# Modulation steps, two weight splits and a memset put elsewhere, and a second power in each layer norm

## Chip, cores and metric

The kernel runs on one core of a Trainium2 chip. The metric is the device time of one execution in microseconds, median of three runs. TensorE (PE) multiplies, with weight loads on PEld; VectorE is DVE, ScalarE is ACT, GpSimd is POOL, and SP is the queue that issues most loads.

## What is computed

Two layers of a first transformer block on 256 tokens of 1024 values, then two layers of a second block on its result and on 256 context tokens. Cut to what matters here, a layer of the first block is:

```python
mod = c_act @ ada_w[l] + ada_b[l]
sh1, sc1, g1, sh2, sc2, g2 = jnp.split(mod, 6, axis=-1)
h = _modulate(x, sh1, sc1)                 # norm of x, times 1 + sc1, plus sh1
mix = _hybrid_mixer(h, ...)                # h @ w_in, attentions, convolution, @ w_o
x = _layer_norm(ALPHA * x + (1.0 + g1) * mix, ln1_g, ln1_b)
h = _modulate(x, sh2, sc2)
ffn = _peer(h, ...)                        # 16384 experts, U and V tables, gates from top-16
x = _layer_norm(ALPHA * x + (1.0 + g2) * ffn, ln2_g, ln2_b)
```

The second block computes its own modulation rows in the same way, from its own `w_ada`.

## The kernel before

A matrix product is made of three products of halves in a rounded fp32 format. `wtile` (line 272) loads a raw weight tile (`raw`, five buffers) on SP and calls `split` (260): ScalarE copies the high half (`wh`, 262), VectorE subtracts it for the low half (`wl`, 264); there are five buffers of each. `mm3` (295 to 297) makes the three products. The code is one program order; a scheduler orders each engine's and each queue's instructions from it by priority (program order) and by its own model of times, so an instruction may be drawn far forward into what the model takes for idle time. On the chip each engine and queue then runs in that fixed order. `tc.issue_after(ins)` holds the instructions made under it behind `ins` on that engine; `PIN` passes such a bound to `split`.

Modulation rows are made in two ways. `ada` (323) multiplies on PE (L342) from loads `adaw` (L334) with four buffers. `ada_v` (381) runs on VectorE: for each of eight row blocks a load (L392, two buffers) and a scaled sum into `adacc` (L396 for the first, L398 for the others), then a finish: a sum over partitions on PE (L404) into the one bank that `ada` uses too, the bias (L412), transposes (L421) and a copy (L425). Each block and the finish are a step of a generator. `behind` (460) holds eleven such parts: one of layer 0, six of layer 1, four of the second block. Its `run(budget)` adds to a debt and takes steps, each worth 1.0, while the debt is above zero.

`peer` (817) computes the experts. Its second half is a loop over V (1033): 64 positions of two experts, first 120 to 126, then 0 to 118 in steps of two. Each position multiplies activations and gates on VectorE (1038), splits them and two V tiles of 1024 columns, and makes 24 products into `acc`, one pair of banks for each of the two token blocks. At the end of each position stands `behind.run`. In layer 0 the products of the last two positions are put off and made token block by token block, so that `resid_ln` (554) can start on the first. `resid_ln` takes for each block: gate (557), residual (558), `ln_stats` (468), two scaled operations (560, 561) into X.

`ln_stats` takes bn_stats of two halves (471), bn_aggr (473), the epsilon (475), and `power` (463), which is a pow on GpSimd (465). There are 16 layer norms in the program: eight in `resid_ln` and eight in `make_hT`.

After `peer(0)` comes `mixer(1)` (565). It clears `krn` (595) and calls `make_hT` (495) for each block: `ln_stats`, `neg_mul` (487, kept as `LATE["dve"]`), xn on ScalarE (509), transposes on PE (515), hf (519, 521) and its split into hh and hl. Then the products `pn` with `w1n` follow (608 to 614), eight row blocks each split at columns 416 and 256, and the products of `ada(2, 0, 0)` are handed out in program order behind them. `krn` is written from L628 on, behind `pn`.

Of the kernel before, what the change touches and what calls it, by code (L numbers as in the profile page):

```python
# [205 lines left out]
def kernel(ctx: ExitStack, tc: tile.TileContext, a: dict, out: bass.AP):  # L206
    nc = tc.nc
    V, SC, T, G, SP = nc.vector, nc.scalar, nc.tensor, nc.gpsimd, nc.sync
# [8 lines left out]
    def pool(name, side=None):  # L217
        return tc.tile_pool(name=name, bufs=1, side=side, reuse_waits="tile")
# [12 lines left out]
    def bank(shape, name, tag):  # L231
        return PP[0].tile(shape, F32, name=name, tag=tag, bufs=PP[1][tag])
# [5 lines left out]
    def cst(name, t=None):  # L238
        o, n = CW[name]
        return (k1 if t is None else t)[:, o:o + n]  # L240

    ident, iota = cst("ident"), cst("iota")
    def x_tile():
        return const.tile([128, 2, D], F32, name="x", tag="x8", bufs=1)
# [10 lines left out]
    def raw_tile(src, shape):  # L255
        r = ring.tile([128] + shape, F32, name="raw", tag="raw", bufs=RAW)
        SP.dma_start(r, src)
        return r

    def split(dst_h, dst_l, src):  # L260
        with after(PIN.get("act")):
            SC.activation(dst_h, src, AF.Copy)  # L262
        with after(PIN.get("dve")):
            return V.tensor_tensor(dst_l, src, dst_h, op=OP.subtract).ins  # L264

    LAST = [None]
    PIN = {}

    def after(ins):
        return tc.issue_after(ins) if ins else ExitStack()  # L270

    def wtile(src, shape, cuts=None, keep=None):


        r = raw_tile(src, shape)
        parts = []
        c0 = 0
        for cut in cuts or [shape[0] // 2] * 2:
            sh = [cut] + shape[1:]
            h, lo = [(keep or ring).tile([128] + sh, F32R, name=nm, tag=nm, bufs=4 if keep else NHL) for nm in ("wh", "wl")]  # L280
            LAST[0] = split(h, lo, r[:, c0:c0 + cut])
            parts.append((h, lo))
            c0 += cut
        return parts
# [9 lines left out]
    def mm3(o, lh, ll, rh, rl, first, last):  # L294
        T.matmul(o, lh, rh, start=first, stop=False)  # L295
        T.matmul(o, lh, rl, start=False, stop=False)  # L296
        T.matmul(o, ll, rh, start=False, stop=last)  # L297
# [139 lines left out]
    def mod_row(dst, blk, l, part, s=0):  # L437
        SP.dma_start(dst, bcast_row(mod(blk, l, part, s), D))
# [21 lines left out]
    behind = Filler(*[ada_v(*key) for key in [(1, 0, 5)] + [(1, 1, i) for i in range(6)] + [(2, 1, i) for i in range(2, 6)]])  # L460


    def power(var, u=""):
        r = small.tile(list(var.shape), F32, name="rstd", tag=f"rstd{var.shape[-1]}{u}")
        G.tensor_tensor(r, var, cst("half").to_broadcast(list(var.shape)), op=OP.pow)
        return r

    def ln_stats(xt, u=""):
        st = small.tile([128, 2, 6], F32, name="st" + u)
        for h in range(2):  # L470
            V.bn_stats(st[:, h], xt[:, 512 * h:512 * h + 512])
        mv = small.tile([128, 2], F32, name="mv" + u)
        V.bn_aggr(mv, st)
        v = small.tile([128, 1], F32, name="ve" + u)
        V.tensor_scalar(v, mv[:, 1:2], LN_EPS, None, op0=OP.add)
        return mv[:, 0:1], power(v, u)
# [6 lines left out]
    LATE = {}  # L483
# [11 lines left out]
    def make_hT(work, xt, kind, scc, shc, hh, hl, t0, tag, bufs=2, act=False):  # L495

        xn = work.tile([128, D], F32, name="xn", tag="xn", bufs=bufs)
        if kind == "ln":
            m, r = ln_stats(xt, "h")
            nb = neg_mul(m, r)  # L500
        else:
            ss = small.tile([128, 1], F32, name="ssh")
            SC.activation(xn, xt, AF.Square, accum_out=ss)
            r = rms_from(ss, D, "h")
        hf = work.tile([128, KB, 128], F32, name="hf", bufs=bufs)
        for h in range(2):
            c = slice(512 * h, 512 * h + 512)
            if kind == "ln":
                LATE["act"] = SC.activation(xn[:, c], xt[:, c], AF.Identity, scale=r, bias=nb).ins
            else:  # L510
                V.tensor_scalar(xn[:, c], xt[:, c], r, None, op0=OP.mult)
            pt = bank([128, 4, 128], "hTp", tag)
            for j in range(4):
                k = 4 * h + j
                LATE["pe"] = T.transpose(pt[:, j], xn[:, 128 * k:128 * k + 128], ident).ins
            for j in range(4):
                k = 4 * h + j
                if j % 2 or act:
                    SC.activation(hf[:, k], pt[:, j], AF.Identity, scale=scc[:, k:k + 1], bias=shc[:, k:k + 1])
                else:  # L520
                    V.tensor_scalar(hf[:, k], pt[:, j], scc[:, k:k + 1], shc[:, k:k + 1], op0=OP.mult, op1=OP.add)
            k = slice(4 * h, 4 * h + 4)
            split(hh[:, k, t0:t0 + 128], hl[:, k, t0:t0 + 128], hf[:, k])
        return hf
# [40 lines left out]
    def mixer(l):  # L565
# [19 lines left out]
        with pool(f"mix{l}") as p:  # L585
# [6 lines left out]
            sbv = p.tile([128, 2, 256], F32, name="sbv")  # L592
            qln = p.tile([128, 2, 384], F32, name="qln")
            krn = p.tile([128, 2, 128], F32, name="krn")
            V.memset(krn, 0.0)
            proj = {n: p.tile([128, 2, S], F32, name="t" + n) for n in ("sq", "sk", "cb", "cc")}
            order = ("cb", "cc", "ch", "sq", "sk")
            ph = sth.enter_context(pool(f"mixh{l}"))
# [2 lines left out]
            with pool(f"mixx{l}") as px:  # L601
                for tb in range(2):
                    make_hT(px, X[0][:, tb], "ln", sc, sh, hh, hl, 128 * tb, "m")
            pat = sth.enter_context(pool(f"mixa{l}"))


            pn = [[bank([128, 512], f"pn{tb}{c}", "m") for c in range(2)] for tb in range(2)]
            for k in range(KB):
                w = wtile(a["w1n"][l, 128 * k:128 * k + 128, :], [672], (416, 256))
                for tb in range(2):  # L610
                    t = slice(128 * tb, 128 * tb + 128)
                    for c, n in enumerate((416, 256)):
                        mm3(pn[tb][c][:, :n], hh[:, k, t], hl[:, k, t], w[c][0][:, :n], w[c][1][:, :n],
                            k == 0, k == KB - 1)
# [107 lines left out]
            for hp in range(2):  # L722
                h = slice(2 * hp, 2 * hp + 2)
# [64 lines left out]
            with banks(f"o{l}", pm=2), pool(f"mixo{l}") as p:  # L788
# [9 lines left out]
                for i, k in enumerate(korder):  # L798
                    w = p.tile([128, 2, 2, 512], F32R, name=f"wok{i}")
# [17 lines left out]
    def peer(l, nxt):  # L817
        sta, ex = AHEAD
        st = ExitStack()
# [10 lines left out]
        with pool(f"topk{l}") as p:  # L830
# [147 lines left out]
            j = 0  # L978
# [47 lines left out]
        def spilled(j):  # L1026
            SP.dma_start(Ws[:, j // 2 % 4], spill[:, j:j + 2])
# [5 lines left out]
        for j in order:  # L1033
            W = gab[:, j // 4 % 2, j % 4:j % 4 + 2] if j >= 120 else Ws[:, j // 2 % 4]
            if j + 6 < 120:
                spilled(j + 6)
            with tc.issue_after(last) if last else ExitStack():
                V.tensor_tensor(W, W, Gt[j // 64][:, :, j % 64:j % 64 + 2].rearrange("p t j -> p j t"), op=OP.mult)
            WH, WL = WHL[:, j // 2 % 2, 0], WHL[:, j // 2 % 2, 1]
            last = split(WH, WL, W)  # L1040
            late = j in order[-2:] and l == 0
            v = [wtile(a["V"][l, :, j + c, :], [1024], keep=kp if late and j == order[-1] else None) for c in range(2)]

            def down(j, c, tb):
                t = slice(128 * tb, 128 * tb + 128)
                WH, WL, v = held[j]
                for n in range(2):
                    mm3(acc[tb][:, n], WH[:, c, t], WL[:, c, t], *v[c][n], j + c == order[0], j + c == order[-1] + 1)

            held[j] = WH, WL, v  # L1050
            if not late:
                for c in range(2):
                    for tb in range(2):
                        down(j, c, tb)
            elif j == order[-1]:
                for tb in range(2):
                    for i in order[-2:]:
                        for c in range(2):
                            down(i, c, tb)
            if j == 30:  # L1060
                X[0] = x_tile()
                for tb in range(2):
                    SP.dma_start(X[0][:, tb], xd[tb])
            if j == 62:
                stg[0].close()
                next(nxt)
            behind.run(0.84 if l == 0 else 0.45)
            if j == 100:
                next(nxt)
                kp = stk.enter_context(pool(f"vk{l}"))  # L1070
                gate = pa.tile([128, D], F32, name="rows2", tag="c")
                mod_row(gate, 1, l, 5)
# [433 lines left out]


    gens = [mixer(0), mixer(1), second()]
    for l in range(L):
        for _ in gens[l]:  # L1510
            pass
        peer(l, gens[l + 1])
# [22 lines left out]
```

## Time and profile before

| | |
|---|---|
| median of three runs | 2835.21 us (2834.38 to 2836.84) |
| profiled execution | 2834.45 us, its span 2832.7 us |
| PE busy | 2747.3 us (97%) |
| DVE busy | 2264.3 us (80%) |
| ACT busy | 1672.6 us (59%) |
| POOL busy | 40.3 us (1%) |

A row of a timeline gives the start and the length in us, engine, line, operation, output and inputs with their shapes, the count, and in brackets the idle time of the engine before it with what ended it. A small q behind an engine's name is its queue of DMA issues. Operations of one engine overlap by about 0.1 us, so a row may start before the one above it has ended.

### The profile page before, as it was taken

Reading aid. Unit: us, or ns where it says so; the run is one execution under the profiler, and the core shown is the slowest. Engines: PE = TensorE matmul, PEld = TensorE weight load, DVE = VectorE, ACT = ScalarE, POOL = GpSimd, SP = SyncE. Lnnn points to the kernel's source line nnn. Section 1 sums busy time; section 2 is a strip of 40 time slices with the busy share of each in tenths; the row PEclk is TensorE's granted clock in tenths of the full one; section 3 lists DMA queues with packets and bytes.
Section 4 is the critical chain, followed back from the end, with each engine's and each line's share of the span. In section 5 each row is a group of like instructions: output and inputs, shape, how many; then the busy total and the mean of one; then the engine's idle time right before and its main releaser. Section 6 shows DMA issues by size and latency. Waiting matters only on the chain.

```text
span 2832.7 us, 52697 instructions
## 1 busy us (share of the span) xinstructions
PE 2747.3 (97%) x18870; PEld 2435.8 (86%) x18870; DVE 2264.3 (80%) x5178; ACT 1672.6 (59%) x3459; POOL 40.3 (1%) x50
## 2 busy tenths in 40 slices
PE   7899999999999999999999999999999999998999
PEld 4689999997888766999999888887769999887997
DVE  5989989888788867899889877889768666577565
ACT  3545569885555454555899655555556655565554
POOL 0000000000000000000000000000000000000000
PEclk9999999999999999999999999999999999999999
DMA  8766766668789886477666887878647565651454
GB/s 317 238 244 229 235 218 201 200 209 297 247 289 323 284 271 242 165 242 232 208 195 196 270 276 244 312 246 279 199 164 241 180 202 187 208 188 60 156 189 162
DMA packets 188256, 640.50 MB, mean 226 GB/s; under 512 B 22468, under 2 KB 23876, under 8 KB 187352
## 3 DMA queue, kind: packets, MB, share of 16 engines
q1 hardware_dynamic: 179352, 605.66, 64.9%
q10 hardware_dynamic: 8640, 31.46, 2.8%
q8 instruction: 148, 2.42, 0.3%
q14 instruction: 116, 0.95, 0.1%
HBM read 600.82 MB, written 34.64 MB: 224 GB/s over the span
## 4 chain that ended last, share of the span: by engine, by line
PE 86%; DVE 7%; DMA 3%; ACT 2%; issue 1%; POOL 0%; SPq 0%; DVEq 0%; POOLq 0%; ACTq 0%
PE pact L295 9%; PE pact L297 8%; PE pact L296 8%; PE acc L296 7%; PE acc L297 7%; PE acc L295 7%; PE po L295 3%; PE po L297 3%; PE po L296 3%; DMA adaw<-in_ada_dram 3%; PE pwu L297 2%; PE pwu L295 2%; PE pwu L296 2%; PE pwg L295 2%; PE pwg L297 2%; PE pwg L296 2%
## 5 line engine op out<-in xcount | busy, mean ns | idle before, releaser
L262 ACT ACTIVATE wh<-raw 128x512 fp32r<-128x512 f32 (+1 forms) x1636 | 1010.8, 627 | 828.8 <-PE acc L297 313.0
L264 DVE TENSOR_TENSOR wl<-raw,wh 128x512 fp32r<-128x512 f32 (+1 forms) x1636 | 1088.8, 683 | 331.3 <-ACT wh L262 326.9
L295 PE MATMUL pact<-hh,wh 128*128 128x256 f32 x2048 | 582.7, 285 | 0.0
L297 PE MATMUL pact<-hh,wl 128*128 128x256 f32 x2048 | 572.9, 280 | 1.4 <-DVE wl L264 1.3
L296 PE MATMUL pact<-hl,wh 128*128 128x256 f32 x2048 | 571.9, 279 | 0.0
L296 PE MATMUL acc<-wl,WHL 128*128 128x512 f32 x1024 | 399.7, 390 | 2.0 <-DVE wl L264 1.9
L295 PE MATMUL acc<-wh,WHL 128*128 128x512 f32 x1024 | 399.4, 390 | 0.0
L297 PE MATMUL acc<-wh,WHL 128*128 128x512 f32 x1024 | 399.0, 390 | 0.0
L297 PEld LDWEIGHTS pact<-hh,wl 128*128 128x128 f32 x2048 | 384.9, 188 | 2.4 <-DVE wl L264 2.4
L296 PEld LDWEIGHTS pact<-hl,wh 128*128 128x128 f32 x2048 | 385.4, 188 | 0.0
L295 PEld LDWEIGHTS pact<-hh,wh 128*128 128x128 f32 x2048 | 385.4, 188 | 0.0
L295 PEld LDWEIGHTS acc<-wh,WHL 128*128 128x128 f32 x1024 | 192.2, 188 | 45.6 <-ACT WHL L262 5.9
L296 PEld LDWEIGHTS acc<-wl,WHL 128*128 128x128 f32 x1024 | 192.2, 188 | 45.6 <-DVE wl L264 5.9
L297 PEld LDWEIGHTS acc<-wh,WHL 128*128 128x128 f32 x1024 | 192.2, 188 | 39.7
L998 ACT ACTIVATE hot<-hot,idxT 128x128 f16<-128x128 f16 x512 | 173.8, 401 | 1.6 <-DVE hot L997 1.2
L997 DVE TENSOR_SCALAR hot<-hot,idxT 128x128 f16<-128x128 f16 x512 | 157.9, 308 | 20.2 <-PE pG L999 20.0
L398 DVE SCALAR_TENSOR_TENSOR adacc<-adaw,c,adacc 128x1024 f32<-128x1024 f32 x98 | 125.1, 1277 | 40.2 <-DMA adaw<-in_ada_dram 40.0
L295 PE MATMUL pwg<-f,wh 128*128 128x256 f32 x512 | 143.9, 281 | 0.0
L297 PE MATMUL pwg<-f,wl 128*128 128x256 f32 x512 | 143.5, 280 | 0.0
L296 PE MATMUL pwg<-f,wh 128*128 128x256 f32 x512 | 143.5, 280 | 0.0
L297 PE MATMUL pwu<-f,wl 128*128 128x256 f32 x512 | 143.1, 279 | 0.2 <-DVE wl L264 0.2
L295 PE MATMUL pwu<-f,wh 128*128 128x256 f32 x512 | 142.8, 279 | 0.0
(475 smaller groups left out, 5129.4 us busy)
## 6 DMA issues: line engine op xcount, KB each, us to landing
raw<-in_U_dram SPq DMA_DIRECT2D x256, 512.0 KB, 3.6
raw<-in_V_dram SPq DMA_DIRECT2D x256, 512.0 KB, 4.4
adaw<-in_ada_dram SPq DMA_DIRECT2D x192, 512.0 KB, 5.7
raw<-in_wg_dram SPq DMA_DIRECT2D x66, 512.0 KB, 3.4
raw<-in_wu_dram SPq DMA_DIRECT2D x66, 512.0 KB, 3.3
raw<-in_wd_dram SPq DMA_DIRECT2D x66, 512.0 KB, 4.0
spill<-gab ACTq DMA_DIRECT2D x60, 512.0 KB, 5.1
Ws<-spill SPq DMA_DIRECT2D x120, 256.0 KB, 4.3
```

The lines of the kernel that those rows point to most:

```text
L262: SC.activation(dst_h, src, AF.Copy)
L264: return V.tensor_tensor(dst_l, src, dst_h, op=OP.subtract).ins
L295: T.matmul(o, lh, rh, start=first, stop=False)
L296: T.matmul(o, lh, rl, start=False, stop=False)
L297: T.matmul(o, ll, rh, start=False, stop=last)
L398: V.scalar_tensor_tensor(t, r, c, t, op0=OP.mult, op1=OP.add)
L997: V.tensor_scalar(B, iota16, i2, g, op0=OP.is_equal, op1=OP.mult)
L998: SC.activation(B2, B, AF.Copy, scale=share)
```

## The change

Three things. In the loop over V no steps of modulation are taken at positions 110 to 118 (five positions, ten experts), and the budget of a position is 0.92 instead of 0.84 in layer 0 and 0.49 instead of 0.45 in layer 1. In the mixer the memset of `krn` waits for the last `neg_mul` in VectorE's order, and in layer 1 so do the VectorE halves of the splits of the first two row blocks of `w1n`. In `ln_stats` a pow of the first bn_stats value is issued behind the first half; nothing reads it.

```diff
@@ ln_stats
         for h in range(2):
             V.bn_stats(st[:, h], xt[:, 512 * h:512 * h + 512])
+            if h == 0:
+
+                power(st[:, 0, 0:1], "w")
@@ mixer
             krn = p.tile([128, 2, 128], F32, name="krn")
-            V.memset(krn, 0.0)
@@
             pat = sth.enter_context(pool(f"mixa{l}"))
+            with after(LATE["dve"]):
+                V.memset(krn, 0.0)
...
             for k in range(KB):
+                if l and k < 2:
+                    PIN["dve"] = LATE["dve"]
                 w = wtile(a["w1n"][l, 128 * k:128 * k + 128, :], [672], (416, 256))
+                PIN.clear()
@@ peer
-            behind.run(0.84 if l == 0 else 0.45)
+            if j < 110 or j >= 120:
+                behind.run(0.92 if l == 0 else 0.49)
```

## Rows read from the trace of the kernel before

**Rows 1.** The page's chain that ended last: share of the span by engine.
```profile
PE 86%; DVE 7%; DMA 3%; ACT 2%; issue 1%; POOL 0%; SPq 0%; DVEq 0%; POOLq 0%; ACTq 0%
```

**Rows 2.** Busy time per stretch: PE, PEld, DVE, ACT, POOL; clock; DMA share; GB/s.
```profile
900.00:920.00 20.00, 20.00 (x90) 16.56 (x89) 18.84 (x27) 10.79 (x19) 0.00 (x0) 1.00 0.93 316
...
1940.00:1960.00 20.00, 19.82 (x162) 19.00 (x160) 19.75 (x35) 12.20 (x26) 3.04 (x2) 1.00 0.70 233
...
990.00:995.00 5.00, 0.00 (x0) 0.00 (x0) 5.00 (x11) 0.00 (x0) 1.33 (x1) 0.94 0.88 266
```

**Rows 3.** Timeline of DVE, end of layer 0's loop over V to mixer 1.
```profile
979.40 1.23 DVE L557 TENSOR_TENSOR rl<-acc,rows 128x1024 f32<-128x1024 f32 x1 [2.50 <-PE acc L297]
...
980.60 0.43 DVE L264 TENSOR_TENSOR wl<-raw,wh 128x256 fp32r<-128x256 f32 x1
...
980.94 1.22 DVE L558 SCALAR_TENSOR_TENSOR rl<-x,rl 128x1024 f32<-128x1024 f32 x1
...
982.08 0.59 DVE L264 TENSOR_TENSOR wl<-raw,wh 128x416 fp32r<-128x416 f32 x1
...
982.58 1.28 DVE L471 BATCH_NORM_STATS2 st<-rl 128x6 f32<-128x512 f32 x2
...
983.77 0.41 DVE L264 TENSOR_TENSOR wl<-raw,wh 128x256 fp32r<-128x256 f32 x1
...
984.74 1.28 DVE L560 SCALAR_TENSOR_TENSOR rl<-rl,mv,lgb 128x1024 f32<-128x1024 f32 x1
...
985.93 0.68 DVE L412 SCALAR_TENSOR_TENSOR abias<-adap,abias 64x512 f32<-64x512 f32 x1
...
989.01 0.27 DVE L595 MEMSET krn<- 128x256 f32 x1
...
992.77 0.69 DVE L396 TENSOR_SCALAR adacc<-adaw,c 128x1024 f32<-128x1024 f32 x1
...
994.76 1.22 DVE L398 SCALAR_TENSOR_TENSOR adacc<-adaw,c,adacc 128x1024 f32<-128x1024 f32 x1
...
999.91 0.16 DVE L487 SCALAR_TENSOR_TENSOR nm<-mvh,rstd 128x1 f32<-128x1 f32 x1 [0.75 <-POOL rstd L465]
...
1002.38 0.85 DVE L521 TENSOR_SCALAR hf<-hTp,mcols 128x128 f32<-128x128 f32 x2 [2.31 <-PE hTp L515]
```

**Rows 4.** Timeline of PE in the same stretch.
```profile
984.42 0.39 PE L297 MATMUL acc<-wh,WHL 128*128 128x512 f32 x1
...
987.94 1.92 PE L342 MATMUL adap<-adaw,cT 128*32 128x512 f32 x16 [0.82 <-DVE mcols L425]
...
995.11 3.63 PE L342 MATMUL adap<-adaw,cT 128*32 128x512 f32 x12 [5.25 <-DMA adaw<-in_ada_dram]
...
1001.69 1.09 PE L515 MATMUL hTp<-k,xn 128*128 128x128 f32 x8
...
1007.27 0.46 PE L295 MATMUL pn<-wh,hh 128*128 128x416 f32 x1
```

**Rows 5.** Timeline of POOL: pow at the gap and at the kernel's end.
```profile
984.97 1.46 POOL L465 TENSOR_TENSOR rstd<-ve,k 128x1 f32<-128x1 f32 x1 [811.50 <-DVE ve L475]
993.66 1.46 POOL L465 TENSOR_TENSOR rstd<-ve,k 128x1 f32<-128x1 f32 x1 [7.24 <-DVE ve L475]
997.38 0.55 POOL L465 TENSOR_TENSOR rstd<-veh,k 128x1 f32<-128x1 f32 x1 [2.26 <-DVE veh L475]
...
2824.72 0.55 POOL L465 TENSOR_TENSOR rstd<-ve,k 128x1 f32<-128x1 f32 x1 [183.20 <-DVE ve L480]
```

**Rows 6.** Timeline of SP's queue in the gap: start, stretch of the issues, their count.
```profile
972.25 12.29 SPq L257 DMA_DIRECT2D raw<-in_w1n_dram  x6
...
989.03 18.71 SPq L334 DMA_DIRECT2D adaw<-in_ada_dram  x12
```

**Rows 7.** Timeline of DVE: modulation steps last before and after the gap.
```profile
962.90 1.27 DVE L398 SCALAR_TENSOR_TENSOR adacc<-adaw,c,adacc 128x1024 f32<-128x1024 f32 x1
...
1041.55 1.28 DVE L398 SCALAR_TENSOR_TENSOR adacc<-adaw,c,adacc 128x1024 f32<-128x1024 f32 x1 [4.03 <-DMA adaw<-in_ada_dram]
```

## The prediction

> **What bounds the kernel now.** I read the page's chain first, then busy time per stretch, then the order of time around the one place that the diff touches most. The chain [rows 1] lies on TensorE for 86% of the span and on VectorE for 7%: what counts is any stretch in which PE has nothing to do, and in those VectorE is the one to look at. In the stretches [rows 2] the loop over V keeps PE at 20.00 of 20 us while VectorE works 18.84, so in the loop's body modulation is hidden. 90 matmuls in 20 us and 24 per position (two experts, two token blocks, two halves, three products) make a position 5.3 us. Layer 1's end of that loop (1940 to 1960) still has 19.82 of PE, because products of the second block fill it. The gap is at layer 0's end: from 990 to 995 PE runs nothing at all, and VectorE is busy all the time.
>
> VectorE's side of that gap is in [rows 3]. It waits 2.50 us for acc of token block 0, starts the residual at 979.40, and from there works without a pause until the last neg_mul (L487) at 999.91; then it idles 2.31 us for the transposes. PE's side is in [rows 4]: the first product of the next mixer (pn) comes at 1007.27, behind transposes at 1001.69. In between it runs products of ada (L342), which come in bursts because they wait for their loads (5.25 us before 995.11). So the chain is acc, two residual norms, two mixer norms, all on VectorE in one queue, then xn, transposes, hf, hh, pn. A microsecond taken out of VectorE between 979.40 and 999.91 is worth about a microsecond of the end, if PE's own queue lets the transposes through.
>
> **Part 1, the run budget.** Nine steps make a part of modulation (eight row blocks, then the finish: L404, L412, L421, L425). Before, step 54, the finish of the sixth part, comes when the sum of budgets passes 53: 53/0.84 = 63.1, position 64, the last one. After, 53/0.92 = 57.6: position 58, six positions or some 32 us earlier. At position 59 the sum is 54.28, so one step of the next part follows; in layer 1 both budgets (28.80 and 28.91) give 29 steps. No work is removed, and the finish takes its two bias loads along, past V loads on SP. The denser budget adds 0.08 of a step to a position, 0.1 us of VectorE (L398 takes 1.28), against 1.16 us free in 20 where steps already run [rows 2]: hidden, 0. What moves out of the gap is the finish: L412 starts at 985.93 for 0.68 us, but fills a wait for POOL (POOL's pow ends at 984.97 + 1.46 = 986.43 [rows 5], L412 at 986.61), so 0.2 us of it counts at most; I take 0.1. The bank that the finish frees counts more: L342 starts at 987.94 [rows 4] only after it, and the row of twelve adaw loads only at 989.03 [rows 6], when L342 frees their buffers. With the bank free since about 950, L342 can start when the loop's last product ends, near 984.8 [rows 4], and loads and products of ada come 3.1 us earlier. They stand ahead of the transposes in PE's queue, so without this a shorter VectorE chain would win little.
>
> The other steps that VectorE runs in the gap are L396 (992.77, 0.69 us) and L398 (994.76, 1.22 us). By the code these belong to the part that starts in layer 1's loop: the scheduler drew them forward by 600 us into what it took for free time, as soon as the accumulator was free. L398 covers a wait for POOL until 993.66 + 1.46 = 995.12 and ends at 995.98, so 0.86 us of it counts. After, the accumulator is free six positions before the end, and the first of these steps is placed in the loop. I expect the same scheduler to put the others into the last positions too: in [rows 7] the loop's last step with a load was at 962.90, so the stretch that the change means to clear was already clear, and may now fill up. There they lie beside PE's products. Price taken: 0.69 + 0.86 = 1.55 us gained; bounds 0 (they are in the gap again) and 1.9 (both durations whole). One step stays to be watched: in the mixer behind the gap L398 waited 4.03 us for its load at the head of VectorE's queue [rows 7]. That is gone if the part is done earlier; I take 0.5 us of it, with 0 and 4.0 as bounds, since softmax work queues behind it.
>
> **Part 2, splits and memset behind the norm.** Three of the four splits sit inside the norm of token block 0: from the split's start to the next start 0.34 us (980.60 to 980.94), 0.50 (982.08 to 982.58) and, by duration, 0.41 (983.77) [rows 3]: 1.25 us. The fourth lies in the 2.50 us wait for acc and gives nothing. The memset gives 0.27. They go behind neg_mul, where two of 0.59 and two of 0.43 with the memset make 2.3 us against 2.31 us of idle time ahead of hf at 1002.38: covered, just. If that idle time shrinks, up to 2.3 us come back; the products need the first split at 1007.27, so I take 0. The ScalarE halves of the splits aren't pinned. What queues behind the pinned ones: the raw buffers of the first two weight blocks stay taken. Before, the sixth load of L257's row was issued at 972.25 + 12.29 = 984.54 [rows 6], when the splits had freed a buffer; after, it and the one before it wait for neg_mul, some 13 us longer. They are needed five blocks after 1007, so by themselves they cost nothing. In layer 0 there is no load to hold back, and the memset moves within idle time: 0.
>
> **Part 3, the second power.** It looks like a warming of POOL: pow takes 1.46 us at 984.97 and 993.66 but 0.55 at 997.38 [rows 5]. The trace speaks against it. After 183.20 us of idle time pow took 0.55 at 2824.72, so it is not rest that makes it slow. The slow ones run beside L560 on VectorE (984.74 to 986.02 [rows 3]) and end 0.41 us after it. The second power doesn't alter that: L560 still starts ahead of the real pow. I take 0 for the sixteen of them. Lower bound: a gain of 0.41 us in each of eight residual norms, 3.3 us, if it were rest after all. Upper bound: each holds VectorE up for its 0.55 us, 8.8 us in all. From bn_stats to the next large operation (L560) there are about 1.1 us, twice the 0.55, so 0 is near.
>
> The Trainium skill (SBUF — State Buffer, section "SBUF: two separate sides") says that GpSimd and a VectorE operation with two SBUF inputs shut each other out for a whole instruction, whichever comes first. The rows of pow agree (1.46 beside L560, 0.55 without). By it the warming gives 0 and the second power could cost instead; that is the fifth case below.
>
> **Sum.** The gap: 1.25 + 0.27 + 0.1 + 1.55 = 3.17, taken as 3.0 for what PE's queue may keep; the mixer 0.5; layer 1's end and the powers 0. Together 3.5 us. The profiled run took 2834.45 us (span 2832.7 and 1.75 around it), 0.76 under the median of 2835.21. 2834.45 - 3.5 = 2830.95, and on the median's footing 2831.7.
>
> **The rivals.**
> - The positions fill up and the gap too: low-priority steps are drawn back between the norms. For it: L396 and L398 stood there before. Left are the splits, the memset and 0.1: 1.6 us, 2833.6.
> - More than that: the gap gives 3.2 us and the 4.03 us stall in the mixer is all on the path: 7.2 us, 2828.0. For it: PE runs nothing from 990 to 995, so there is room. Against: PE is nearly full in that part of the mixer, so a stall of VectorE there is mostly hidden.
> - Slower: the sixth and seventh weight loads stand in SP's queue ahead of adaw loads and wait for neg_mul. All that is behind them waits too, and the ada products stand ahead of the transposes on PE. Place: SP at 985 to 1000. Price: loads issued at 989.03 fed PE at 995.11, 6.1 us; issued behind the pinned splits, at about 999, they feed a burst of 3.63 us from 1005 on [rows 4], and the transposes come near 1008.7 instead of 1001.69: 7 us over the median, 2842.2. It decides if two or more of the twelve adaw loads stand behind a pinned weight load.
> - The second power does warm: 3.3 us more, 2828.4. Against: 0.55 us after 183.20 us.
> - The second power blocks VectorE: 8.8 us at most on the forecast, 2840.5. Against: 1.1 us of room each.
>
> **How the numbers follow.** Forecast 0.43, filled up 0.20, larger gain 0.22, SP's queue 0.10, warming 0.03, blocking 0.02. From these: a measurement of this kernel can tell about 0.2% (5.7 us) from no change, so faster means under 2829.5 and slower over 2840.9. Faster: 0.22 + 0.03 = 0.25. Slower: 0.10 and 0.01 of the blocking case's tail, 0.11. Within: 0.64. The range takes in the larger gain and the loss of all gain with a few us of reordering elsewhere: 2826.5 to 2839.5; the SP case is left out.
>
> **What would show it.** Right: in the changed trace L404 comes some 30 us before the loop's end, L342 starts within 1 us of the loop's last product, no split stands between 979 and the last neg_mul, pn starts 3 us sooner after the loop's last product (984.8 to 1007.27 is 22.5 us before), and pow still takes 1.46 beside L560. Filled up: L398 between the residual norms. SP's queue: an adaw load issued after a w1n load that waited for wl. Wrong altogether if the loop over V itself grows, because modulation at 0.92 makes VectorE late for the products, or if the end moves by more than the gap did.

## Result and profile after

The changed kernel takes 2851.99 us (median of 6 runs, 2847.29 to 2857.03) against 2834.83 for the kernel before on the same chip: the ratio is 1.0056, with a 95% interval of 1.0044 to 1.0068. It is slower by 17 us, where 3.5 us less were forecast. The profiled execution took 2849.32 us (span 2847.5). Its mean granted clock is 0.991 against 0.989, so the clock is not the cause.

The page's chain by engine, after, answers to [rows 1]:

```profile
PE 88%; DVE 5%; DMA 3%; ACT 2%; issue 1%; POOL 0%; SPq 0%; DVEq 0%; POOLq 0%; ACTq 0%
```

VectorE's share of the chain fell from 7 to 5%, and PE's rose from 86 to 88%. PE got more to do, though not one product was added. The page's groups of products show where. `pact` are the products of the first half of `peer` (moving operand `hh` or `hl`, weights `wh` or `wl`), `acc` those of its loop over V (moving operand `wh` or `wl`, weights `WHL`). First before, then after (line, engine, operation, output<-moving operand and weights by the program's names, shapes, count; busy us and mean ns of one; idle time before):

```profile
L295 PE MATMUL pact<-hh,wh 128*128 128x256 f32 x2048 | 582.7, 285 | 0.0
L297 PE MATMUL pact<-hh,wl 128*128 128x256 f32 x2048 | 572.9, 280 | 1.4 <-DVE wl L264 1.3
L296 PE MATMUL pact<-hl,wh 128*128 128x256 f32 x2048 | 571.9, 279 | 0.0
L296 PE MATMUL acc<-wl,WHL 128*128 128x512 f32 x1024 | 399.7, 390 | 2.0 <-DVE wl L264 1.9
L295 PE MATMUL acc<-wh,WHL 128*128 128x512 f32 x1024 | 399.4, 390 | 0.0
L297 PE MATMUL acc<-wh,WHL 128*128 128x512 f32 x1024 | 399.0, 390 | 0.0
```

```profile
L295 PE MATMUL pact<-hh,wh 128*128 128x256 f32 x2048 | 586.8, 287 | 0.0
L297 PE MATMUL pact<-hh,wl 128*128 128x256 f32 x2048 | 575.3, 281 | 1.2 <-DVE wl L264 1.2
L296 PE MATMUL pact<-hl,wh 128*128 128x256 f32 x2048 | 575.5, 281 | 0.0
L295 PE MATMUL acc<-wh,WHL 128*128 128x512 f32 x1024 | 403.5, 394 | 0.0
L297 PE MATMUL acc<-wh,WHL 128*128 128x512 f32 x1024 | 402.0, 393 | 0.0
L296 PE MATMUL acc<-wl,WHL 128*128 128x512 f32 x1024 | 399.7, 390 | 1.5 <-DVE wl L264 1.3
```

With the same shapes and counts, five of the six lines take 1 to 4 ns longer for each product. These two kinds fill more than half of the span. Busy times of pipelined products overlap, so I add up the intervals from one product's start to the next instead (those under 1 us): the three lines of pact together go from 735.2 to 741.6 us, the three of acc from 702.3 to 710.1. That is 6.4 + 7.8 = 14.2 us of the 14.8 by which the span grew.

Cut at the first or last product of each stretch, the profiled executions differ like this (us; "places as before" is the change with its tiles moved back, run e3 below). Each column is one execution, and executions of one kernel lie some us apart, so small differences are readings and not tests:

| stretch | before | after | places as before |
|---|---|---|---|
| pact of both layers, until the first acc | 794.58 | +6.37 | +0.54 |
| loop over V of both layers | 712.89 | +6.92 | +3.26 |
| gap: end of layer 0's last acc to first pn | 22.46 | -2.72 | -1.46 |
| pn products of mixer 1 | 14.85 | +2.32 | +2.32 |
| last pn to the mixer's last output product | 99.10 | -3.91 | -1.54 |
| from there to layer 1's first pact | 66.84 | +3.92 | +5.61 |
| everything else | 1121.9 | +2.0 | +0.2 |

So there are two stories: products that run slower all through the experts, which the prediction did not have, and the gap, which came out shorter by nearly what was forecast, while the pn products behind it took 2.32 us more.

**The gap.** The chain of waits inside it, before (start, us, what):

```profile
986.61 1.19 DVE x L561
...
987.94 1.09 PE adap L342 x8
989.03 6.04 DMA adaw<-in_ada_dram
...
995.11 1.95 PE adap L342 x4
...
997.08 3.59 DMA adaw<-in_ada_dram
...
1000.71 1.04 PE adap L342 x2
1001.75 1.03 PE hTp L515 x8
```

and after:

```profile
992.61 0.23 PE acc L297
992.84 1.06 PE adap L342 x8
...
994.28 6.35 DMA adaw<-in_ada_dram
...
1000.68 1.90 PE adap L342 x4
...
1002.60 4.95 DMA adaw<-in_ada_dram
...
1007.59 1.05 PE adap L342 x4
1008.64 1.02 PE hTp L518 x8
```

In both kernels the second half of the gap hangs on loads of `adaw` and the products that use them, not on VectorE. After, the first product of ada follows the last acc at once (992.84), where before it waited for VectorE until 987.94, over 3 us. Then come the same two waits for loads, together 1.67 us longer than before (11.30 against 9.63).

VectorE's queue after, in the same stretch, answers to [rows 3]:

```profile
984.14 2.60 DVE L398 SCALAR_TENSOR_TENSOR adacc<-adaw,c,adacc 128x1024 f32<-128x1024 f32 x2
987.38 1.23 DVE L560 TENSOR_TENSOR rl<-acc,rows 128x1024 f32<-128x1024 f32 x1 [0.64 <-PE acc L297]
...
991.11 1.27 DVE L398 SCALAR_TENSOR_TENSOR adacc<-adaw,c,adacc 128x1024 f32<-128x1024 f32 x1
...
999.74 1.23 DVE L398 SCALAR_TENSOR_TENSOR adacc<-adaw,c,adacc 128x1024 f32<-128x1024 f32 x1
...
1002.27 1.23 DVE L398 SCALAR_TENSOR_TENSOR adacc<-adaw,c,adacc 128x1024 f32<-128x1024 f32 x1
...
1007.40 0.16 DVE L490 SCALAR_TENSOR_TENSOR nm<-mvh,rstd 128x1 f32<-128x1 f32 x1 [0.73 <-POOL rstd L465]
1007.57 0.27 DVE L608 MEMSET krn<- 128x256 f32 x1
```

Line numbers of the norms are 3 higher than before, those of the experts 7 higher. No split and no memset stands between the norms any more. In their place are three steps of L398 of the next part, where before there were L396 and one L398: the cleared room filled up. From the end of the last acc to the start of the last neg_mul VectorE takes 14.6 us after (992.84 to 1007.40) and 15.1 before (984.81 to 999.91), so its own queue became only 0.5 us shorter.

GpSimd after, answers to [rows 5]:

```profile
990.74 0.55 POOL L465 TENSOR_TENSOR rstd<-st,k 128x1 f32<-128x1 f32 x1 [817.27 <-DVE st L471]
992.76 1.52 POOL L465 TENSOR_TENSOR rstd<-ve,k 128x1 f32<-128x1 f32 x1 [1.47 <-DVE ve L478]
...
2839.61 0.55 POOL L465 TENSOR_TENSOR rstd<-ve,k 128x1 f32<-128x1 f32 x1 [183.56 <-DVE ve L483]
```

The second power takes 0.55 us after 817 us of rest, and the real one behind it still takes 1.52, beside L563 (L560 of before) on VectorE, which starts at 992.60.

### The profile page after: what moved, and what is told of

Same layout as the page of the kernel before. It is cut to its first block, busy times and chain, and to the rows that moved or that the text cites. A ratio compares the mean times of both kernels' runs of the same rounds, so it can differ in the third digit from the quotient of the medians.

```text
span 2847.5 us, 52692 instructions
## 1 busy us (share of the span) xinstructions
PE 2763.2 (97%) x18870; PEld 2440.8 (86%) x18870; DVE 2267.7 (80%) x5178; ACT 1676.2 (59%) x3459; POOL 47.5 (2%) x66
## 4 chain that ended last, share of the span: by engine, by line
PE 88%; DVE 5%; DMA 3%; ACT 2%; issue 1%; POOL 0%; SPq 0%; DVEq 0%; POOLq 0%; ACTq 0%
PE pact L295 9%; PE pact L297 8%; PE pact L296 8%; PE acc L295 8%; PE acc L297 8%; PE acc L296 8%; PE po L295 3%; PE po L297 3%; PE po L296 2%; DMA adaw<-in_ada_dram 2%; PE pwu L297 2%; PE pwu L296 2%; PE pwu L295 2%; PE pwg L295 2%; PE pwg L297 2%; PE pwg L296 2%
## 5 line engine op out<-in xcount | busy, mean ns | idle before, releaser
L295 PE MATMUL pact<-hh,wh 128*128 128x256 f32 x2048 | 586.8, 287 | 0.0
L297 PE MATMUL pact<-hh,wl 128*128 128x256 f32 x2048 | 575.3, 281 | 1.2 <-DVE wl L264 1.2
L296 PE MATMUL pact<-hl,wh 128*128 128x256 f32 x2048 | 575.5, 281 | 0.0
L295 PE MATMUL acc<-wh,WHL 128*128 128x512 f32 x1024 | 403.5, 394 | 0.0
L297 PE MATMUL acc<-wh,WHL 128*128 128x512 f32 x1024 | 402.0, 393 | 0.0
L296 PE MATMUL acc<-wl,WHL 128*128 128x512 f32 x1024 | 399.7, 390 | 1.5 <-DVE wl L264 1.3
L297 PEld LDWEIGHTS pact<-hh,wl 128*128 128x128 f32 x2048 | 385.7, 188 | 2.2 <-DVE wl L264 2.0
L296 PEld LDWEIGHTS pact<-hl,wh 128*128 128x128 f32 x2048 | 386.5, 189 | 0.0
L295 PEld LDWEIGHTS pact<-hh,wh 128*128 128x128 f32 x2048 | 385.8, 188 | 0.0
L296 PEld LDWEIGHTS acc<-wl,WHL 128*128 128x128 f32 x1024 | 192.2, 188 | 48.0 <-DVE wl L264 5.6
L295 PEld LDWEIGHTS acc<-wh,WHL 128*128 128x128 f32 x1024 | 192.4, 188 | 45.8 <-ACT WHL L262 5.9
L297 PEld LDWEIGHTS acc<-wh,WHL 128*128 128x128 f32 x1024 | 192.3, 188 | 43.4
L398 DVE SCALAR_TENSOR_TENSOR adacc<-adaw,c,adacc 128x1024 f32<-128x1024 f32 x98 | 125.4, 1279 | 28.1 <-DMA adaw<-in_ada_dram 27.8
L297 PE MATMUL pwu<-f,wl 128*128 128x256 f32 x512 | 143.7, 281 | 0.2 <-DVE wl L264 0.2
L295 PE MATMUL pwg<-f,wh 128*128 128x256 f32 x512 | 143.9, 281 | 0.0
L297 PE MATMUL pwg<-f,wl 128*128 128x256 f32 x512 | 143.6, 280 | 0.0
L296 PE MATMUL pwg<-f,wh 128*128 128x256 f32 x512 | 143.5, 280 | 0.0
L295 PE MATMUL pwu<-f,wh 128*128 128x256 f32 x512 | 143.5, 280 | 0.0
```

Source lines behind the costliest of these rows:

```text
L398: V.scalar_tensor_tensor(t, r, c, t, op0=OP.mult, op1=OP.add)
```

## Experiments

The theory after the result: the second power costs through the tile that it writes. `rstd1w` is a new tag in the pool `small`, and it takes two buffers of 32 B in each partition. By the places that the compiled program gives its tiles, everything allocated behind that pool from the low end lies 64 B higher, among it the ring of five buffers each of `raw`, `wh` (first one from 48832 to 48896) and `wl`; tiles allocated from the high end stay (`hh` 203744, `WHL` 212160). So the distance between the two operands of a product changes by 64 B, for acc (`wh`, `wl` with `WHL`) and for pact (`hh`, `hl` with `wh`, `wl`). The rivals: the changed order (parts 1 and 2), or the powers' own time.

**e1: parts 1 and 2 without the power.** The diff of the change less this piece:

```diff
-            if h == 0:
-
-                power(st[:, 0, 0:1], "w")
```

> The changed kernel without the second power (parts 1 and 2 alone); its tiles lie where they lay before. Two theories of the 17 us. Place: the power's result tile takes 2 x 32 bytes in the pool of small tiles, and all that is placed behind it, the weight halves wh and wl among them, moves up by 64 bytes against the tiles at the upper end (hh, hl, WHL), and each product takes longer. Order: the denser modulation, the pinned splits and the powers put the work in a worse order. Place expects 2832 (the gap's 3 us gained), acc L295 at a mean of 390 ns as before. Order expects 2845 or more.

Measured: 2841.41 us against 2835.39, ratio 1.0019 (1.0007 to 1.0030). Without the power most of the loss is gone, and the intervals of the products are those of before (pact 734.8, acc 703.2 us). But the 2832 us that place led to expect weren't reached: the two other parts are no gain, and by the interval a loss of at least 2 us.

**e2: the kernel before, its tiles 64 B higher.**

```diff
-    mcols = const.tile([128, 192], F32, name="mcols")
+    mcols = const.tile([128, 208], F32, name="mcols")
```

The added columns are never used; every engine's instructions and their order are those of before.

> The kernel before, unchanged but for a constant tile (mcols) that is made 64 bytes wider, so that all small tiles and all behind them move up by 64 bytes as in the changed kernel; each engine's order of instructions is that of before. Place expects 2849 (+14: acc products 394, 390, 393 ns, pact 287, 281, 281). Order expects 2835, no change.

Measured: 2849.97 us, ratio 1.0053 (1.0036 to 1.0070). The loss is there with no other change than the places. The pact products take what they took after: 741.6 us of intervals.

**e3: the change, its tiles back where they were.**

```diff
-    mcols = const.tile([128, 192], F32, name="mcols")
+    mcols = const.tile([128, 176], F32, name="mcols")
```

> The changed kernel whole, second power included, with the same constant tile 64 bytes narrower (16 columns that nothing uses), so that the weight halves lie where they lay before. Place expects 2832 to 2835, acc L295 at 390 ns. Order expects 2850 as the changed kernel.

Measured: 2838.70 us, ratio 1.0012 (1.0000 to 1.0023). All that the change does is in it, and 13.3 of its 17 us are gone. Intervals: pact 735.6, acc 703.1 us, as before. The time is still over the 2832 to 2835 us expected.

**e4: the second power alone, tiles where they were** (the piece of e1's diff added to the kernel before, with `mcols` at 176 columns).

> The kernel before with the second power alone, and the same constant tile 64 bytes narrower, so that places are those of before. Place expects 2835 (the powers themselves cost and gain nothing: pow beside L560 stays at 1.46 to 1.53 us). That powers cost by themselves expects 2840 or more; that they warm GpSimd expects 2832 and a pow of 0.55 beside L560.

Measured: 2836.35 us, ratio 0.9999 (0.9990 to 1.0009). The sixteen powers cost nothing and bring nothing: pow in the residual norms still takes 1.45 to 1.53 us.

**e5: the budget alone**, and **e6: the held splits and the memset alone.**

```diff
-            behind.run(0.84 if l == 0 else 0.45)
+            if j < 110 or j >= 120:
+                behind.run(0.92 if l == 0 else 0.49)
```

> The kernel before with the run budget of the change alone (0.92 and 0.49, none at positions 110 to 118); places as before. The run without the power lost 6 us instead of gaining 3: the gap at layer 0's end was shorter, but ada's products of the second half stood ahead of the transposes after mixer 1, and PE stalled in layer 1's loop over V. If the budget makes both, this run takes 2840 or so and shows L342 with a wait for its load between 1120 and 1130 and PE under 10.00 of 10 us at 1800 to 1850. If the pinned splits make them, it takes 2833 to 2835.

```diff
-            V.memset(krn, 0.0)
...
+            with after(LATE["dve"]):
+                V.memset(krn, 0.0)
...
+                if l and k < 2:
+                    PIN["dve"] = LATE["dve"]
                 w = wtile(a["w1n"][l, 128 * k:128 * k + 128, :], [672], (416, 256))
+                PIN.clear()
```

> The kernel before with the pinned splits and the memset alone; places as before. If these only shorten the norm chain in the gap, as forecast, it gains 1.5 us: 2834. If they cost what the budget does not, 2838 to 2841.

Measured: e5 2835.95 us, ratio 1.0005 (0.9994 to 1.0017); e6 2835.39, 1.0008 (0.9996 to 1.0020). Neither makes a difference that can be measured. Their traces show why. In e6 the gap is 2.02 us shorter and the pn products behind it 2.32 us longer. PE's queue there:

```profile
1005.25 0.45 PE L295 MATMUL pn<-wh,hh 128*128 128x416 f32 x1
...
1006.05 1.04 PE L342 MATMUL adap<-adaw,cT 128*32 128x512 f32 x2
1007.03 0.57 PE L297 MATMUL pn<-wh,hl 128*128 128x416 f32 x2
...
1009.24 1.05 PE L342 MATMUL adap<-adaw,cT 128*32 128x512 f32 x2
```

Products of ada that stood ahead of pn before now stand in between: two pieces of about 1 us. The start of pn moved, its end did not.

In e5 the gap is 1.50 us longer, not shorter. ada's first product follows the last acc at once (985.93), but the two waits for its loads in the chain grow from 6.04 and 3.59 to 6.38 and 6.75 us. The finish has a price on PE too. Before, its eight products (L404 and L421) stood in the gap; now they stand in the loop, where PE is full. The first four, after:

```profile
957.69 0.40 PE L297 MATMUL acc<-wh,WHL 128*128 128x512 f32 x1
958.01 1.05 PE L404 MATMUL adap<-adacc,k 128*32 128x512 f32 x4
959.00 0.50 PE L295 MATMUL acc<-wh,WHL 128*128 128x512 f32 x1
```

From one acc to the next it takes 1.31 us instead of 0.23, and 0.70 around the four of L421 (960.36): 1.55 us more in all. With the intervals into and out of them, the products other than acc take 6.0 us of layer 0's loop in before and e6, and 8.1 in e1, e3, e5 and after.

In e5 the stretch from pn to the mixer's last output product is 3.19 us shorter, and the one behind it 5.21 us longer. PE's queue at that place, first before, then e5:

```profile
1127.68 1.92 PE L342 MATMUL adap<-adaw,cT 128*32 128x512 f32 x4 [0.54 <-DMA adaw<-in_ada_dram]
1129.54 1.75 PE L515 MATMUL hTp<-k,xn 128*128 128x128 f32 x8
1131.20 2.06 PE L493 MATMUL pwq<-hf,raw 128*128 128x128 f32 x15
```

```profile
1127.26 3.22 PE L342 MATMUL adap<-adaw,cT 128*32 128x512 f32 x8 [4.67 <-DMA adaw<-in_ada_dram]
1130.41 0.90 PE L515 MATMUL hTp<-k,xn 128*128 128x128 f32 x3
1131.24 1.54 PE L342 MATMUL adap<-adaw,cT 128*32 128x512 f32 x4
...
1133.52 1.05 PE L342 MATMUL adap<-adaw,cT 128*32 128x512 f32 x4
...
1136.32 1.05 PE L342 MATMUL adap<-adaw,cT 128*32 128x512 f32 x4
...
1138.16 1.05 PE L342 MATMUL adap<-adaw,cT 128*32 128x512 f32 x4
```

Four more pieces of ada, about 1 us each, stand among the transposes and the products of the next gap. The transposes themselves start 1.3 us later behind the mixer's last product than before, because the wait for loads ahead of them is 4.67 us instead of 3.02 and 0.54. PE runs in this order, so the stretch behind mixer 1 takes what the mixer had gained.

**e7: the change, with the distance of acc alone put right.** `WHL` moves 192 B down, so that it is again a whole number of 256 B from `wh`; `hh` stays.

```diff
-        WHL = pa.tile([128, 2048 + SHIFT + 8], F32R, name="WHL", tag="hb")[:, SHIFT:SHIFT + 2048]
+        WHL = pa.tile([128, 2048 + SHIFT + 8], F32R, name="WHL", tag="hb")[:, 8:2056]
```

> The changed kernel whole; only the halves WH and WL start 192 bytes lower within their tile, so that wh and WHL are a multiple of 256 bytes apart again, as before the change (they are 64 bytes off it in the changed kernel). If the distance of the two operands sets a product's time, acc goes back to 390 ns in all three lines and some 7 us of the loss goes: 2844. pact, whose operands are not moved, stays at 287, 281, 281. If it is the place of wh alone, nothing changes: 2851.

Measured: 2847.54 us, ratio 1.0051 (1.0033 to 1.0068). The median is 4.5 us lower than that of the change, but the ratios, 1.0051 and 1.0056, can't be told apart; 2844 was expected. What e7 shows is in its trace: acc's intervals fell by 7.0 us, to 703.1, and the groups of acc are back at 390 ns:

```profile
L296 PE MATMUL acc<-wl,WHL 128*128 128x512 f32 x1024 | 399.6, 390 | 1.4 <-DVE wl L264 1.3
L295 PE MATMUL acc<-wh,WHL 128*128 128x512 f32 x1024 | 399.6, 390 | 0.0
L297 PE MATMUL acc<-wh,WHL 128*128 128x512 f32 x1024 | 399.1, 390 | 0.0
```

`wh` is still where the change put it, so its own address was not the trouble for acc; the distance to `WHL` was.

**e8: the kernel before, 32 B up, with `WHL` moved up too.** acc keeps its distance and pact comes to a multiple of 256 B.

```diff
-    mcols = const.tile([128, 192], F32, name="mcols")
+    mcols = const.tile([128, 200], F32, name="mcols")
...
-        WHL = pa.tile([128, 2048 + SHIFT + 8], F32R, name="WHL", tag="hb")[:, SHIFT:SHIFT + 2048]
+        WHL = pa.tile([128, 2048 + SHIFT + 8], F32R, name="WHL", tag="hb")[:, SHIFT + 8:SHIFT + 2056]
```

> The kernel before with the constant tile 32 bytes wider and WHL 32 bytes higher within its tile. Then wh and WHL are a multiple of 256 bytes apart as before, and wh and hh too (32 bytes off it before). By distance acc stays at 390 ns and pact falls from 285, 279, 280 to about 279 each: 2830 to 2833. By the place of wh alone both lose some 3 us each: 2841.

Measured: 2860.05 us, ratio 1.0092 (1.0068 to 1.0115). My expectation was the wrong way round: the multiple of 256 B, best for acc, is the worst place seen for pact (749.7 us of intervals, 14.5 more than before).

**e9 to e12: the kernel before, all moved by 128, 32, -32 and 256 B** (`mcols` at 224, 200, 184 and 256 columns, nothing else).

> The kernel before with one constant tile 128 B wider, so that everything behind it (the ring's raw, wh, wl) lies 128 B higher and the tiles on the right side stay; instructions and their order are those of before. Theory (the distance between a product's two operands sets its pace): acc goes from a multiple of 256 B to 128 B off it and is slower by as much as at 64 B or more, 228 to 234 ns instead of 227, pact goes from 32 B below the other operand to 160 B (96 above modulo 256), unknown, between 117 and 120 ns; 2840 to 2855 us. Rival (only the shift by 64 B was unlucky, as an address, not a distance): 2835.

> The kernel before with one constant tile 32 B wider: acc is 32 B off a multiple of 256 B, pact at a multiple of 256 B. With the V loop's copy of the left operand moved along (a run ahead of this) the same shift gave 2860, 25 us more, with acc at 227 ns. Theory: pact costs the same 14 us or so again, and acc adds up to 8 us of its own: 2850 to 2868 us. Rival (the 25 us came from moving the V loop's operand tile, not from pact's distance): 2835 to 2842.

> The kernel before with one constant tile 32 B narrower: everything behind it lies 32 B lower. acc is 32 B off a multiple of 256 B on the other side, pact 64 B from its other operand. Theory: acc between 227 and 234 ns, pact between 117 and 120 ns; 2835 to 2850 us. It would be under 2833 only if one of the two likes its new distance better than the one it has. Rival (only upward shifts cost): 2835.

> The kernel before with one constant tile 256 B wider: all distances change by a whole 256 B. Theory (distance modulo 256 B decides): acc stays at 227 ns, pact at its 117 ns, and the time stays that of before, 2834 to 2837 us. Rival (any shift costs, or the absolute place does): 2845 to 2855 us.

Measured: e9 2861.36 us, ratio 1.0082 (1.0062 to 1.0101); e10 2876.35, 1.0140 (1.0123 to 1.0157); e11 2854.38, 1.0070 (1.0044 to 1.0096); e12 2835.64, 0.9992 (0.9983 to 1.0002). The groups of acc, line 295, of e10 and then of e12:

```profile
L295 PE MATMUL acc<-wh,WHL 128*128 128x512 f32 x1024 | 405.4, 396 | 0.0
```

```profile
L295 PE MATMUL acc<-wh,WHL 128*128 128x512 f32 x1024 | 399.6, 390 | 0.0
```

A shift of 32 B costs 40 us and one of 256 B nothing. e9, e10 and e11 are all slower than the ranges expected for them, which counted acc and pact alone. In e10 the terms add up: 16.5 us more in acc, 14.5 in pact, 8.0 in the second block's experts (pwg and pwu), 39.0 of the 40. All of it in one table, with the intervals from one execution each (that of e11, 2845.11 us, is the fastest of four that reach to 2862.72): the distance of the operands modulo 256 B (place of the moving operand less that of the weights: `wh` less `WHL` for acc, `hh` less `wh` for pact), the median interval between starts, and the sum of the three lines.

| kernel | acc: B | ns (L295, L296, L297) | us | pact: B | ns (L295, L296, L297) | us | median us |
|---|---|---|---|---|---|---|---|
| before | 0 | 227, 227, 227 | 702.3 | 32 | 117, 117, 117 | 735.2 | 2834.83 |
| e12 | 0 | 227, 227, 227 | 701.9 | 32 | 117, 117, 117 | 734.9 | 2835.64 |
| e3 | 0 | 227, 227, 227 | 703.1 | 32 | 117, 117, 117 | 735.6 | 2838.70 |
| e7 | 0 | 226, 227, 227 | 703.1 | 224 | 117, 117, 117 | 741.6 | 2847.54 |
| e8 | 0 | 227, 227, 227 | 701.9 | 0 | 120, 120, 120 | 749.7 | 2860.05 |
| after | 64 | 232, 226, 229 | 710.1 | 224 | 118, 117, 117 | 741.6 | 2851.99 |
| e2 | 64 | 229, 231, 226 | 707.2 | 224 | 118, 117, 117 | 741.6 | 2849.97 |
| e9 | 128 | 232, 232, 232 | 716.5 | 160 | 119, 118, 119 | 742.0 | 2861.36 |
| e11 | 224 | 234, 234, 234 | 719.4 | 64 | 118, 118, 118 | 738.7 | 2854.38 |
| e10 | 32 | 234, 234, 234 | 718.8 | 0 | 120, 120, 120 | 749.7 | 2876.35 |

Rows with the same distance have the same pace, whatever the order of the instructions (e3 and before; after and e2 within 3 us), and for acc whatever the address (e7 and e8, where both operands moved). For pact only the weights were ever moved, so these rows alone don't tell their distance from their address. Other products of its shape do: in e8, by the places of the program, all pwg and pwu products have weights at 224 B modulo 256, and they start every 120 ns (median) where the moving operand lies at 224 B too and every 118 ns where it lies at 0, 32 B off. No layout tried is faster than that of the kernel before beyond the noise, and so no version beats it.

## Why the prediction was wrong

**The step that failed is part 3**, "I take 0 for the sixteen of them". Its three bounds (3.3 us gained, 0, 8.8 lost) all price the instruction's time, and by that measure it was right: e4 gives 0.9999, pow keeps 1.52 us beside its VectorE neighbour, and neither warming nor blocking happened. What was not priced is the tile that the instruction writes. It moved the ring by 64 B, and that moved the pace of 9,200 products: 13.3 us by e3 against the change, 14.6 by e2 against before. The rows put on record don't show that a place has a price, but the trace of before has it, in two groups of one shape in the second block:

```profile
L297 PE MATMUL po<-wh,b 128*128 128x512 f32 x88 | 34.2, 389 | 0.0
L297 PE MATMUL po<-wh,mix 128*128 128x512 f32 x80 | 31.7, 396 | 0.0
```

The moving operand is `wh` in both; by the places of the program it lies 0 B from `b` and 224 B from `mix`, modulo 256. In e10, where it comes to lie 32 B from `b`, that group takes 395 ns. The code hints at it too: `WHL` is cut out of its tile at an offset called SHIFT, which has no other use than its place. Every change that adds or resizes a tile should have had a rival "all products at another pace", with a size unknown. The range was too narrow for want of it. The signs named for "right" didn't help: all of them came true in the slower kernel, or nearly (pn 2.72 us sooner), because they look at the gap, the finish and pow alone. The sign for "wrong altogether", a loop over V that grows, came true as well (6.9 us), but not by a late VectorE: PE's waits for `wl` in acc fell (2.0 to 1.5 us), and what grew is the products' pace and, by 1.55 us, the finish in the loop.

**The reading of the bound** was right for the loop and half wrong for the gap. "A microsecond taken out of VectorE between 979.40 and 999.91 is worth about a microsecond" holds only up to 987.94. From there on the chain runs through loads of adaw and products of ada to the transposes, as the chain above shows for the kernel before itself. I had the two rows for this in [rows 4] (5.25 us before 995.11) and [rows 6], and weighed them as a limit on the gain and not as the bound.

**Part 1.** The finish moved to 958.01, 34 us before the loop's last product, as worked out (32). ada's first product starts 0.32 us behind the start of the last acc (992.45 to 992.77) instead of 3.52: 3.2 us, where 3.1 were worked out. In e5, where this part stands alone, the same 3.2 us are there and pn still starts 1.5 us later: the loads took them back. What the finish costs PE in the loop, 1.55 us, was put at nothing, since only VectorE's time in the loop was priced. The 1.55 us for L396 and L398 were wrong, for two reasons: they weren't on the chain, and three such steps came back into the gap, which is the sign named for the rival "the positions fill up". The 4.03 us stall of [rows 7], taken at 0.5, is gone after, and that stretch of the mixer is 3.9 us shorter. That the one made the other is not shown: in e5 a step of L398 still waits there for 2.82 us, and the stretch is 3.2 us shorter all the same. Either way the gap at the mixer's end takes 5.2 us (e5) and 3.9 us (after) more, which no part of the text had.

**Part 2.** 1.52 us were expected of the splits and the memset. The gap alone is 2.0 us shorter in e6, and the pn stretch 2.3 longer, because products of ada moved from the one into the other. The step "the products need the first split at 1007.27, so I take 0" missed that PE's queue would be made anew around the later splits. The held weight loads came later than the 13 us worked out, too: the one issued at 984.54 before, 0.3 us ahead of the last acc's end, and the one ahead of it come 22 and 18 us behind that end after (1015.09 and 1011.23). That cost nothing by itself, as forecast: no pn product waits.

**Sum of the gap:** 3.0 forecast, 2.72 measured until pn's start, 0.40 until its end. That 3.0 and 2.72 are near each other is luck. ada's earlier start gave 3.2, which the forecast had as a condition and not as a term, and 0.5 was lost behind it (19.33 us from ada's start to pn's before, 19.81 after); the terms of the sum lay on VectorE, whose queue became 0.5 us shorter.

**The rivals.** The slower one named a real thing in the wrong place. In the gap of layer 0 no adaw load waited behind a held weight load: ten of the twelve are issued from 993.86 on, right behind the products that free their buffers, and the last two stand behind weight loads (1012.67 and 1015.51) but later than pn's start at 1012.58. At the next gap, products of ada stand ahead of the transposes and among them. The price there was 5.2 us in e5, of which 3.2 had been gained just before, and not 7; most of it is PE's own time for the added pieces.

**What stays open.** e1 is 2.0 to 8.5 us slower by its interval, e5 and e6 by 1.4 and 2.3 us in the middle of intervals that reach from a gain of 2 to a loss of 6. Whether the two parts together lose more than each alone is not settled. In e1's profiled run 4 us of the loss lie in the V loops. 1.4 of them are in layer 0, about what the finish costs there. The other 2.6 are in layer 1; the longest hold, 1.65 us at 1806.9, is a wait for a split behind a step of L398 that waited 1.79 us for its load. Whether that is regular isn't shown.

## What to carry to other kernels

A small tile is not free because its instruction is: where tiles are laid out one behind the other, it moves every tile behind it. Before reading a change's effect, compare the busy time of groups of instructions that the change doesn't touch. If products of the same shape and count have another mean, pad the tiles back to their places and measure again; one unused column block does it.

Around a gap, follow the chain through it row by row before pricing the engine that looks busy. And when a stretch gets shorter, look at the next two: the queue of a fixed-order engine fills up with what was waiting.

## What the runs showed of the hardware

The pace of back-to-back products at the full granted clock depends on the distance in bytes between the places of their two operands within a partition, modulo 256 B, as far as the layouts tried go. The products of acc, with 512 moving columns, start every 227 ns at a distance of 0, every 226 to 232 ns at 64 B, 232 at 128 B and 234 at 32 B to either side. Those of pact, with 256 columns, start every 117 ns at 32 B, 118 at 64 B, 120 at 0, and 117 to 119 at 160 and 224 B with longer sums (742 against 735 us). A shift by a whole 256 B changes nothing (e12). The pace of acc follows the distance and not the address of `wh` (e7, e8); for 256 columns this rests on pwg and pwu in e8 (120 ns at 0, 118 at 32 B). What makes it so, and why the best distance is another one for the two kinds, stays open: no run separates the weight load from the product that streams beside it.

The Trainium skill (SBUF — State Buffer, section "SBUF: two separate sides") says that on the engines' side only the port shared by GpSimd and VectorE causes waits, and that PE never waits on anyone. The runs agree on pow (0.55 us alone, 1.52 beside a VectorE operation with two inputs). On PE they show a pace that changes by about 3% (227 to 234 ns) with nothing changed but the places of its operands. Whether that is a wait on another engine, which the section rules out, no run here shows.
